# Loading the fourth opening tile of a in one transfer instead of two

## The chip, the cores and the metric

The kernel runs on one core of one Trainium2 chip. The metric is the device time of one execution in microseconds (us); lower is better. Beside the timed runs there is one execution taken by the hardware profiler. Its page and its trace are what is read here: TensorE is PE (its weight loads PEld), VectorE is DVE, ScalarE is ACT, GpSimd is POOL and SyncE is SP. "SPq" is SyncE's queue, from which most plain transfers are issued.

## The reference

With a of 1024 x 1024, b of 1024 x 2048 and c of 2048 x 1024, all float32:

```python
h = np.matmul(a, b)
h = 0.5 * h * (1 + np.tanh(np.sqrt(2 / np.pi) * (h + 0.044715 * h ** 3)))
return np.matmul(h, c).astype(np.float32)
```

Two matrix products with the tanh form of GELU between them.

## The kernel before

The schedule is written by hand: each engine executes its instructions in the order in which the program text issues them to it. A tile has 128 partitions. TensorE contracts over the partitions, so a has to be turned: k on the partitions, rows of a along the free axis (aT). The hidden matrix h is kept turned as well, n on the partitions.

**Opening.** This is where the diff lies. `load_a0(mt, parts)` (L66) allocates a float32 tile of 128 rows and 1024 columns of a (512 KB, 4 KB a row) and loads it from SyncE's queue in `parts` column slices (L70). It is called for the first four row tiles, mt = 0 to 3 (L81). `load_b0(k, parts)` (L73) loads one slice of b: 128 rows of k and the first 1024 columns, also 512 KB, also from SyncE (L77); it is called for all eight k (L83), slice 0 in two halves. The pool for a has four buffers, that for b six, so slices 6 and 7 of b wait until the casts of slices 0 and 1 have freed a buffer. On GpSimd a small copy `gate` (L86) reads slice 4 of b; GpSimd's own loads follow it in that engine's order.

While the loads run, TensorE does `warm_up` matmuls on zeros (L93). `cast_a0(mt)` (L97) makes bfloat16 of a tile: VectorE does columns 0 to 511 (L99), ScalarE columns 512 to 1023 (L100). `turn0(mt, ...)` (L103) transposes the tile in two groups of four 128 x 128 blocks on TensorE (L107) into one of two PSUM buffers `pt`, and copies each group into aT: group 0 on VectorE (L110), group 1 on ScalarE (L112). The order around it is what matters here:

```python
    ab = [cast_a0(0)]
    for mt in R:
        if mt < 3:
            ab.append(cast_a0(mt + 1))
        turn0(mt, ab[mt], (0,) if mt == 3 else (0, 1))
        if mt < 3:
            warm_up(3)
    cast_b0(0)
```

So on VectorE the cast of tile 3 stands ahead of the copy of tile 2's first group, and that copy has to free its `pt` buffer before the first group of tile 3 can be transposed. Group 1 of tile 3 is turned only after the first k group of matmuls.

`cast_b0(k)` (L116) makes bfloat16 of a slice of b, the left 512 columns on VectorE (L117), the right 512 on ScalarE (L118). Then, for each k, six matmuls (L132) add to six PSUM banks: the first 512 rows of a times the first 768 columns of b. All matmuls of one k need slice k.

**The rest.** The six banks go through GELU on ScalarE (L138). GpSimd's queue loads the second half of a, the other columns of b and then c (L150 to L155, L251). The remaining tiles of the first 1024 columns of h are computed plainly (L174 and L167, with more transposes at L160). The last 1024 columns of h, and then all of the second product, use sums and differences of quarter matrices, seven block products in place of eight; those products run in `prod` (L233), with the sums made on VectorE (L197 to L220, L241, L349), ScalarE and by accumulating transfers. Stores go out from SyncE (L345). None of this is touched by the diff.

Of the kernel before, what the change touches and what calls it, by code (L numbers as in the profile page):

```python
# [19 lines left out]
def kernel(ctx, tc, a, b, c, out):  # L20
# [45 lines left out]
    def load_a0(mt, parts):  # L66
        st = astage.tile([128, K], F32, name="a_st")
        w = K // parts
        for i in range(parts):
            nc.sync.dma_start(out=st[:, ts(i, w)], in_=av[:, mt, ts(i, w)])  # L70
        a_st[mt] = st
# [7 lines left out]

    gate = consts.tile([128, 1], F32, name="gate")  # L80
    for mt in R:  # L81
        load_a0(mt, 2 if mt == 3 else 1)
    for k in range(KT):  # L83
        load_b0(k, 2 if k == 0 else 1)

# [349 lines left out]
```

## Time and profile before

| | us |
|---|---|
| median of 4 runs | 121.59 |
| lowest and highest run | 120.63, 122.12 |
| the profiled execution, its whole time | 121.55 |
| its span, from first to last instruction | 119.8 |
| TensorE busy in the span | 112.5 (94%) |
| VectorE busy | 81.7 (68%) |
| ScalarE busy | 46.3 (39%) |

Starts in the trace are counted from the beginning of the span. A row of the timeline gives start, duration, engine, line, operation, out<-in with the shapes, and in brackets how long the engine had been idle before it and which event ended that. Rows that follow each other on one engine can be merged (x3); ends of pipelined instructions are modelled, so neighbours may overlap a little. The "chain that ended last" is followed back from the last instruction: at each step to what released it, or to the instruction before it on its engine.

Some more durations that the steps use: the L70 and L77 issues take 0.33 to 0.81 us each on SyncE's queue (most 0.44), and the transfers of a land 3.4 to 6.3 us after their issue, those of b 6.5 to 9.8 us.

### The profile page before, as it was taken

How to read it: one execution, taken by the hardware profiler on the slowest of the kernel's cores; microseconds unless marked ns; L12 is line 12 of the kernel's file. 1: busy time of each engine (PE TensorE's matmuls, PEld its weight loads, DVE VectorE, ACT ScalarE, POOL GpSimd, SP SyncE). 2: the span in 40 equal slices, each digit the busy share in tenths (PEclk: the TensorE clock that was granted, in tenths of full speed). 3: DMA queues.
4: the chain of work that ended last, by engine and by line, in shares of the span. 5: the costliest groups of instructions: out<-in, count | busy, mean ns of one | idle time of the engine just before them, and what ended most of it. 6: DMA issues, size and time to landing. Idle time of an engine off the chain costs nothing.

```text
span 119.8 us, 1587 instructions
## 1 busy us (share of the span) xinstructions
PE 112.5 (94%) x579; PEld 75.4 (63%) x585; DVE 81.7 (68%) x111; ACT 46.3 (39%) x77; POOL 26.6 (22%) x39
## 2 busy tenths in 40 slices
PE   6966799999999999999999999999999999999990
PEld 2343344469844444788888446888888888886470
DVE  0353233045999945999999999995789992834350
ACT  4355545876533365505359999412000000000000
POOL 2000049923300000066504248200006500000000
PEclk9999999999999999999999999999999999999999
DMA  3999999999999999929999999999997999854434
GB/s 112 369 359 348 419 416 196 188 356 384 215 206 208 206 208 386 321 63 245 257 238 207 190 200 198 183 200 152 149 169 159 242 263 345 327 189 174 167 114 157
DMA packets 13831, 28.41 MB, mean 237 GB/s; under 512 B 1024, under 2 KB 5504, under 8 KB 13824
## 3 DMA queue, kind: packets, MB, share of 16 engines
q0 software_dynamic: 9216, 17.83, 72.3%
q1 hardware_dynamic: 4464, 10.42, 23.3%
q8 instruction: 4, 0.07, 0.2%
q10 hardware_dynamic: 144, 0.07, 0.2%
q14 instruction: 3, 0.02, 0.0%
HBM read 20.97 MB, written 4.19 MB: 210 GB/s over the span
## 4 chain that ended last, share of the span: by engine, by line
PE 86%; DMA 7%; SPq 2%; issue 1%; DVE 1%
PE ps L233 63%; PE ps L174 10%; PE ps L132 8%; DMA b_st<-in_b_dram 7%; PE ps L167 4%; SPq L70 2%; PE pt L160 1%; SPq L77 1%; DVE b_lo L117 0%; DVE ot L404 0%
## 5 line engine op out<-in xcount | busy, mean ns | idle before, releaser
L233 PE MATMUL ps<-t,s 128*128 128x512 f32 x64 | 14.9, 392 | 0.0
L233 PE MATMUL ps<-c,h 128*128 128x512 bf16 (+2 forms) x78 | 14.1, 336 | 0.1
L233 PEld LDWEIGHTS ps<-t,s 128*128 128x128 f32 x64 | 12.0, 188 | 2.6
L174 PE MATMUL ps<-aT,b_lo 128*128 128x512 bf16 x54 | 12.5, 379 | 0.1
L138 ACT ACTIVATE h<-ps 128x512 bf16<-128x512 f32 (+2 forms) x19 | 9.4, 537 | 8.2 <-PE ps L174 6.1
L241 DVE TENSOR_TENSOR ot<-ps,v 128x512 f32<-128x512 f32 x16 | 10.4, 685 | 3.1 <-PE ps L233 3.1
L132 PE MATMUL ps<-aT,b_lo 128*128 128x512 bf16 x47 | 10.7, 379 | 1.6 <-DVE b_lo L117 1.5
L138 ACT ACTIVATE h<-ot 128x512 bf16<-128x512 f32 (+1 forms) x16 | 9.4, 623 | 5.9 <-DVE ot L241 5.9
L233 PE MATMUL ps<-t,h 128*128 128x512 f32 x48 | 11.7, 389 | 0.0
L233 PEld LDWEIGHTS <-h 128*128 128x128 bf16 x80 | 7.1, 98 | 7.0 <-issue 0.5
L349 DVE TENSOR_TENSOR ot<-ps,p 128x512 f32<-128x512 f32 x11 | 7.5, 688 | 5.5 <-PE ps L233 3.1
L233 PEld LDWEIGHTS ps<-t,h 128*128 128x128 f32 x48 | 9.0, 188 | 1.9
L174 PEld LDWEIGHTS <-b_lo 128*128 128x128 bf16 x56 | 5.4, 98 | 6.2
L132 PEld LDWEIGHTS <-b_lo 128*128 128x128 bf16 x48 | 4.4, 98 | 7.2 <-DVE b_lo L117 3.4
L117 DVE CAST b_lo<-b_st 128x512 bf16<-128x512 f32 x8 | 3.4, 426 | 7.0 <-DMA b_st<-in_b_dram 7.0
L251 POOL DMA_DIRECT2D c<-in_c_dram x8 | 6.4, 844 | 6.0 <-DMA b<-in_b_dram 3.8
L233 PE MATMUL ps<-as,bt 128*128 128x512 f32 x32 | 7.6, 396 | 0.0
L233 PE MATMUL ps<-as,b 128*128 128x512 f32 x32 | 7.4, 389 | 0.0
L233 PE MATMUL ps<-c,s 128*128 128x512 f32 x32 | 7.4, 389 | 0.0
L118 ACT ACTIVATE b_lo<-b_st 128x512 bf16<-128x512 f32 x8 | 5.0, 630 | 5.4 <-DMA b_st<-in_b_dram 5.4
L233 PE MATMUL ps<-aT,bx 128*128 128x512 bf16 x31 | 7.0, 379 | 0.1
L382 POOL DMA_DIRECT2D t<-c x4 | 3.5, 1042 | 15.3 <-PE ps L233 14.3
(66 smaller groups left out, 167.2 us busy)
## 6 DMA issues: line engine op xcount, KB each, us to landing
out_dram<-ot SPq DMA_DIRECT2D x15, 256.0 KB, 2.1
b_st<-in_b_dram SPq DMA_DIRECT2D x7, 512.0 KB, 9.0
c<-in_c_dram POOLq DMA_DIRECT2D x6, 512.0 KB, 17.8
t<-c POOLq DMA_DIRECT2D x6, 512.0 KB, 6.7
b<-in_b_dram POOLq DMA_DIRECT2D x2, 1024.0 KB, 10.7
c<-in_c_dram POOLq DMA_DIRECT2D x2, 1024.0 KB, 20.2
t<-t POOLq DMA_DIRECT2D x4, 512.0 KB, 8.6
a_st<-in_a_dram SPq DMA_DIRECT2D x3, 512.0 KB, 4.3
```

What stands on the lines that cost most here:

```text
L70: nc.sync.dma_start(out=st[:, ts(i, w)], in_=av[:, mt, ts(i, w)])
L117: nc.vector.tensor_copy(b_lo[:, k, 0:HW], b_st[k][:, 0:HW])
L118: nc.scalar.activation(b_lo[:, k, HW:W0], b_st[k][:, HW:W0], AF.Copy)
L132: nc.tensor.matmul(ps[t], b_lo[:, k, ts(t, 128)], aT[0][:, k, :], start=(k == 0), stop=(k == KT - 1))
L138: nc.scalar.activation(dst, src, AF.Gelu_apprx_tanh)
L167: nc.tensor.matmul(p, b_lo[:, k, ts(t, 128)], aT[1][:, k, ts(q, 256)], start=(k == 0), stop=(k == KT - 1))
L174: nc.tensor.matmul(p, b_lo[:, k, ts(t, 128)], aT[h][:, k, :], start=(k == 0), stop=(k == KT - 1))
L233: nc.tensor.matmul(p, lhs(t)[:, ts(j, 128)], rhs(t)[:, q], start=(t == 0), stop=(t == n - 1))
L241: tt(ot, p, u, op=ADD)
L251: nc.gpsimd.dma_start(out=dst[:, t:t + 4, :], in_=cv[:, r * NH + t:r * NH + t + 4, ts(q, H)])
L349: tt(ot, p, u, op=ADD)
L382: nc.gpsimd.dma_start(out=t2[i], in_=c21[:, P2[i], :], accum_op=ADD)
```

## The change

Tile 3 of a is loaded by one transfer of 512 KB with rows of 4 KB, where it was loaded by two of 256 KB with rows of 2 KB. The first slice of b is still loaded in two halves. SyncE issues four transfers for a in place of five; nothing else in the text of the kernel differs.

```diff
     gate = consts.tile([128, 1], F32, name="gate")
     for mt in R:
-        load_a0(mt, 2 if mt == 3 else 1)
+        load_a0(mt, 1)
     for k in range(KT):
         load_b0(k, 2 if k == 0 else 1)
```

## The prediction

> **What bounds the kernel now.** I read the chain that ended last first, then the same chain in order of time, then the timeline from 7.5 to 10.9 us and after it, and last the table by stretches.
>
> ```profile
> PE 86%; DMA 7%; SPq 2%; issue 1%; DVE 1%
> ```
>
> The chain is TensorE for 86% of the span. The rest is almost all in the opening, which the same chain shows in order of time (start, us, what):
>
> ```profile
> 4.00 0.04 issue
> 4.05 8.65 DMA b_st<-in_b_dram
> 12.70 0.02 issue
> 12.72 0.44 DVE b_lo L117
> 13.16 0.05 issue
> 13.21 9.24 PE ps L132 x42
> 22.45 0.43 PE ps L174 x2
> ```
>
> The transfer issued at 4.05 is slice 1 of b (load_b0(1)). It lands at 12.70, its first half is cast on VectorE, and from 13.21 TensorE runs to 119 with gaps of some 0.05 us. So the end moves only if slice 1, or a slice behind it, moves, or if TensorE gets to its second k group later than 13.21 for another reason. 42 matmuls take 9.24 us, so one group of six takes 1.32 us. The slices behind slice 1 arrive every 1.27 us (their casts begin at 14.01, 15.27, 16.55, 17.83 and 19.10). Slice 2 would be ready for TensorE at 14.49, group 2 begins at 13.21 + 1.32 = 14.53: the slices keep a lead of 0.04 us that grows by 0.05 per group. Hence a shift of the whole stream moves the end one for one, and a shift of slice 1 alone by at most 0.04.
>
> The other path into the first group is that of tile 3 of a, which the diff touches (start, us, engine, line, ..., idle before and its releaser):
>
> ```profile
> 7.57 0.43 DVE L99 CAST ab<-a_st 128x512 bf16<-128x512 f32 x1 [1.35 <-DMA a_st<-in_a_dram]
> 7.91 0.42 DVE L110 COPY aT<-pt 128x512 bf16<-128x512 bf16 x1
> ...
> 8.25 0.43 DVE L99 CAST ab<-a_st 128x512 bf16<-128x512 f32 x1
> ...
> 8.80 0.42 DVE L110 COPY aT<-pt 128x512 bf16<-128x512 bf16 x1
> ...
> 8.91 0.63 ACT L100 ACTIVATE ab<-a_st 128x512 bf16<-128x512 f32 x1 [0.22 <-DMA a_st<-in_a_dram]
> 8.96 0.81 PE L93 MATMUL ps<-warm 128*128 128x512 bf16 x3
> ...
> 9.60 0.39 PE L107 MATMUL pt<-ident,ab 128*128 128x128 bf16 x4
> 10.03 0.42 DVE L110 COPY aT<-pt 128x512 bf16<-128x512 bf16 x1 [0.80 <-PE pt L107]
> 10.37 0.42 DVE L117 CAST b_lo<-b_st 128x512 bf16<-128x512 f32 x1
> ...
> 10.84 0.39 PE L132 MATMUL ps<-aT,b_lo 128*128 128x512 bf16 x1 [0.85 <-DVE b_lo L117]
> ```
>
> Tile 2 is cast from 7.57; the first half of tile 3 on VectorE at 8.25 and its second half on ScalarE at 8.91, each 0.03 after its landing (8.22 and 8.88: the records of landing, 6.1 and 6.3 us after the issues at 2.12 and 2.59). The first k group starts at 10.84, and with the four transposes behind it TensorE is through at 12.54. Then it waits 0.67 us for slice 1. That wait is the cover of everything done on tile 3's path.
>
> **Part 1: one issue less on SyncE's queue.** Five L70 issues start every 0.47 us from 0.74; dropping one brings each b issue forward by 0.47 us until waits take over. But the queue is far ahead of the data: slice 1 is issued at 4.05 and lands 8.65 later, behind transfers that are already queued. Value on the path: 0. It would count only if the DMA engines ran dry; their busy share is 1.02 to 1.05 in most stretches of one microsecond from 3 to 16 us, and 0.91 and 0.92 from 5 to 7.
>
> **Part 2: larger rows.** Half a tile moves rows of 2 KB, a whole one rows of 4 KB. From tile 2 to the second half of tile 3 the ScalarE casts step from 7.57 to 8.91, 1.34 us for 512 KB in two halves; whole slices of b step by 1.27. So one transfer saves 1.34 - 1.27 = 0.07 us of engine time, and all eight slices, which queue behind it, land 0.07 earlier. This is on the path: -0.07. Here the Trainium skill (DMA: Bandwidth & Descriptors, "Anatomy of one DMA") would promise more: a transfer costs a fixed part of about 2.0 us beside its bytes (it gives this for transfers that GpSimd issues), so one fewer would save up to 2 us if they ran one behind the other. The rows show the halves landing 0.66 apart, far below 2: the fixed part lies under the neighbours' data. By the rule -2.0, by the rows -0.07; I take the rows.
>
> **Part 3: the first half of tile 3 comes later.** The cast L99 waited for half the tile and will wait for all of it. Tile 2's cast began at 7.57, so tile 3's begins at 7.57 + 1.27 = 8.84 in place of 8.25: 0.59 later. Behind it on VectorE, in its own order, is the copy L110 of tile 2, which frees the PSUM buffer for tile 3's transposes. Step by step: L99 at 8.84; L110 0.34 behind (as 7.57 to 7.91): 9.18; done after 0.42: 9.60; transposes 0.05 later (as L110's end at 6.22 to PE at 6.27): 9.65, where the three warm-up matmuls had kept TensorE until 9.60 anyway; L110 of tile 3 after 0.43 (9.60 to 10.03): 10.08; the cast of slice 0 after 0.34: 10.42; the first matmul after 0.47 (10.37 to 10.84): 10.89. The 0.59 shrinks to 0.05 at the first group, and ScalarE's half comes 0.07 earlier (8.84), as does its cast of slice 0's second half (10.95 to 10.88). First group and transposes end by 12.59, and slice 1 is ready at 13.21 - 0.07 = 13.14: 0.55 us of cover are left. Value: 0; without cover, +0.05.
>
> **Part 4: the semaphores shift by one.** The trace's records of SyncE show eight landing semaphores in turn. The ninth and later transfers wait for the one eight before: slice 3 (issued 5.45) for tile 1, slice 4 (7.56) for tile 2, slice 5 (8.24) for the first half of tile 3. With one transfer fewer, slices 3, 4 and 5 wait for tiles 0, 1 and 2 instead, about 0.9, 2.1 and 0.7 us earlier. What is queued behind each on SyncE is only the next slice. Slices 6 and 7 still wait for the casts of slices 0 and 1 to free buffers (issues at 11.61 and 13.38), now 0.07 earlier at most. Slice 4 lands at 16.5, 9 us after its issue, so the wait wasn't what kept it. Its worth is bounded from both sides: if the idle 9% of the engines from 5 to 7 us came from too few queued transfers, 2 x 0.09 = 0.18 us are to be had; if more queued transfers get in each other's way, as much is lost. I take 0, for the engines had six whole transfers ahead of them then. GpSimd's gate (L86) waits for slice 4 and so its loads start 0.07 earlier; none of them ended a wait on TensorE from 22.5 to 119.
>
> **Sum.** -0.07 on the path. The profiled execution took 121.55 us (119.8 of span and 1.75 around it), so 121.48; it lies 0.04 under the median of the runs, 121.59, so 121.52: **121.5 us**.
>
> **Rivals.**
>
> 1. *It gets slower through VectorE's order* (15 in 100). From 4.6 to 7.1 and from 9.0 to 11.3 us many transfers go slowly (GB/s falls to 289 to 330 from some 420). The second spell delays slice 1: it came 1.77 us behind slice 0's second half, 0.50 over the usual step, and that half itself came 1.38 behind the first, 0.70 over. Were that 1.2 us not lost, slice 1 would be ready at 12.0, and tile 3's path decides: TensorE would enter the second group at 12.54 before and 12.59 now, +0.05 against a kernel that had the same luck, 121.6. The switch is at slice 1 ready before 12.59. Against it: it was ready at 13.16 here.
> 2. *More transfers queued early fill the engines* (12 in 100): slices 0 and 1 come 0.2 to 0.6 earlier; 0.55 of cover and 0.07 set the limit, so 120.9 to 121.3.
> 3. *A slow spell falls differently* (11 in 100). One more spell costs what one cost here, 0.6 to 1.2 us: 122.1 to 122.7, and nothing of the change itself would show.
> 4. *The clock falls* (4 in 100). The Trainium skill (TensorE: Matmul & The Clock Gate, "What's actually happening") speaks against anything that makes TensorE wait early: after an idle window of about 3.4 us the clock halves. The row shows waits of 0.85 before the first group and 0.67 after it, a granted clock of 1.00, and this change adds 0.05 to one. By the rule as a threshold: nothing. Were it to happen, a window of 3.4 us at half speed loses 1.7 us: 123.2.
>
> **How the numbers follow.** The forecast itself has 58 in 100, at 121.5, with 121.2 to 121.9 as its own range for the scatter of runs (120.63 to 122.12 singly). For 8 in 10 the range takes in rival 2 from 120.9 and most of rival 3, to 122.4. About 1% is what a measurement of this kernel can tell from no change, 120.4 to 122.8 here. Beyond the upper end lie rival 4 and the worst of rival 3, 0.06; beyond the lower end only rival 2 with luck in the runs, 0.03; within it 0.91.
>
> **What would show each step.** Part 2: L117 for slice 1 at about 12.65, the slices still 1.27 apart, L132's long run from 13.14. Part 3: L99 for tile 3 beside L100 at about 8.84, the transposes L107 at 9.65, the first L132 at 10.89 and TensorE's idle before the second group 0.5 to 0.6. Part 4: L77 issues of slices 3 to 5 at about 4.6, 5.5 and 7.6. The forecast is wrong if the second group starts more than 0.3 from 13.14, or if TensorE shows waits after 22 us that it doesn't show now.

## The result, and the profile after

The changed kernel takes 121.94 us (median of 44 runs, 121.27 to 122.67), the kernel before 121.57 us (63 runs, 120.63 to 122.21). The ratio is 1.0032, with a 95% interval of 1.0020 to 1.0045: slower by about 0.39 us, where the forecast was 0.07 faster. The time lies inside the range that was stated, which was made wide for the scatter of runs and for slow spells; the direction was wrong.

The profiled execution of the changed kernel took 121.58 us, with a span of 119.8; it lies in the quicker quarter of its runs, and so hides the loss. Its chain in order of time (start, us, what) is the one of before, and slice 1 of b still sets the start of TensorE's long run:

```profile
3.60 9.10 DMA b_st<-in_b_dram
12.71 0.02 issue
12.73 0.44 DVE b_lo L117
13.17 0.05 issue
13.22 9.24 PE ps L132 x42
```

Slice 1 is issued 0.45 us earlier than before, as the dropped issue lets it, and lands at the same time: 9.10 us under way in place of 8.65. The timeline of the changed kernel shows the tiles:

```profile
8.00 0.43 DVE L99 CAST ab<-a_st 128x512 bf16<-128x512 f32 x1 [1.99 <-DMA a_st<-in_a_dram]
8.34 0.42 DVE L110 COPY aT<-pt 128x512 bf16<-128x512 bf16 x1
...
9.28 0.63 ACT L100 ACTIVATE ab<-a_st 128x512 bf16<-128x512 f32 x1 [0.17 <-DMA a_st<-in_a_dram]
9.28 0.43 DVE L99 CAST ab<-a_st 128x512 bf16<-128x512 f32 x1 [0.53 <-DMA a_st<-in_a_dram]
...
9.63 0.42 DVE L110 COPY aT<-pt 128x512 bf16<-128x512 bf16 x1
...
11.34 1.47 PE L132 MATMUL ps<-aT,b_lo 128*128 128x512 bf16 x5 [0.85 <-DVE b_lo L117]
...
13.22 2.98 PE L132 MATMUL ps<-aT,b_lo 128*128 128x512 bf16 x13 [0.19 <-DVE b_lo L117]
```

Tile 3's two casts now begin together, 1.28 us after tile 2's, and the first k group 2.06 us behind them, as the steps had it. But tile 2 itself came 0.43 us later than before, so the wait for slice 1 is 0.19 us, not the 0.55 foreseen. That goes with the execution and not with the change: tile 2 landed at 7.98 us in this one and at 7.52 in e1, the same kernel again, where the wait is 0.65; in two executions of the opening of before it landed at 7.54 and 7.90 (before and e3).

One profile says little about a loss of 0.3%. What can be read from all of them is where the time is decided. In six profiled executions (three of the opening of before, three of that of after, with e1, e3, e4 and e12 from below) the time less the start of the second k group is the same within 0.1 us:

| execution | slice 1 lands | second group starts | time | time less start |
|---|---|---|---|---|
| before | 12.70 | 13.21 | 121.55 | 108.34 |
| e12, before again | 12.55 | 13.06 | 121.43 | 108.37 |
| e3, before, halves swapped | 12.75 | 13.26 | 121.58 | 108.32 |
| after | 12.71 | 13.22 | 121.58 | 108.36 |
| e1, after again | 12.83 | 13.34 | 121.71 | 108.37 |
| e4, after, copies first | 13.04 | 13.54 | 121.95 | 108.41 |

So all that differs happens before the second group, and in all six slice 1 was what it waited for. A difference of 0.37 us between the medians then stands for a slice 1 that comes 0.37 us later. This is worked out from the table; no single profile shows the median execution, and the means of the three profiles each differ by half as much, 0.19 us (slice 1 at 12.67 and 12.86). Two of the other kernels below don't fit the column: e7 and e8 have 108.76 and 108.75. In e7 TensorE waited a second time, at 25 us, 0.23 us for a tile of a from GpSimd's queue; e8 lost its 0.4 after VectorE's last instruction.

Where the transfers lose it is in the table by stretches. Columns are the stretch, its length, the busy time of each engine, the granted clock, the busy share of the DMA engines and GB/s. The kernel before:

```profile
6.00:7.00 1.00, 0.73 (x9) 0.62 (x10) 0.22 (x1) 0.58 (x2) 0.00 (x0) 1.00 0.92 289
7.00:8.50 1.50, 0.78 (x7) 0.31 (x5) 0.93 (x3) 0.93 (x2) 0.00 (x0) 1.00 1.04 397
8.50:11.50 3.00, 2.15 (x18) 1.18 (x17) 1.36 (x4) 1.85 (x4) 0.00 (x0) 1.00 1.00 343
4.50:11.50 7.00, 4.92 (x40) 2.82 (x41) 3.19 (x9) 4.23 (x8) 0.00 (x0) 1.00 0.98 340
```

The changed kernel:

```profile
6.00:7.00 1.00, 0.94 (x10) 0.68 (x10) 0.01 (x1) 0.36 (x1) 0.00 (x0) 1.00 1.02 401
7.00:8.50 1.50, 0.45 (x3) 0.02 (x1) 0.50 (x2) 0.50 (x1) 0.00 (x0) 1.00 1.03 273
8.50:11.50 3.00, 1.83 (x16) 1.17 (x17) 1.77 (x5) 2.23 (x5) 0.00 (x0) 1.00 0.97 294
4.50:11.50 7.00, 4.49 (x39) 2.63 (x39) 3.04 (x8) 3.96 (x8) 0.00 (x0) 1.00 0.97 309
```

The stretch from 6 to 7 us, where most of tile 3 is moved, is cured: 401 GB/s in place of 289. The next two are worse: 273 for 397 and 294 for 343. They move the end of tile 3, slice 0's halves and the beginning of slice 1. The engines are as busy as before (last column but one), and slices 1 to 3 are issued by 5.62 us, so packets take longer and none is missing for want of issues. The trace's records of single packets show it: most packets of 2 KB take 84 ns, and of those that began from 7 to 11.5 us, over 100 ns took 9 of 433 in before, 10 of 414 in e12 and 30 of 413 in e3, but 72, 70 and 50 of 256 in after, e1 and e4 (the larger totals include packets of tile 3's halves).

Over the seven microseconds from 4.5 to 11.5 the three executions with the opening of before moved 340, 346 and 342 GB/s, those with the opening of after 309, 307 and 337: on average 25 GB/s less, 0.175 MB in 7 us, and at the 418 GB/s that follow, 0.42 us. That is of the size of the loss, but it doesn't follow it from one execution to the next: e4, with 337, has the latest slice 1 of the six. One reason can be seen. The trace records each landing sixteen times, once for each DMA engine, and the cast of slice 1 begins 0.02 us after the last; that last engine lay 1.85 us behind the first in before and 1.43 in after.

### The profile page after: what moved, and what is told of

It reads as the page before. It is cut to its first block, busy times and chain, and to the rows that moved or that the text cites. A ratio compares the mean times of both kernels' runs of the same rounds, so it can differ in the third digit from the quotient of the medians.

```text
span 119.8 us, 1586 instructions
## 1 busy us (share of the span) xinstructions
PE 112.6 (94%) x579; PEld 75.5 (63%) x585; DVE 81.5 (68%) x111; ACT 46.3 (39%) x77; POOL 26.6 (22%) x39
## 4 chain that ended last, share of the span: by engine, by line
PE 86%; DMA 8%; SPq 2%; DVE 1%; issue 1%
PE ps L233 63%; PE ps L174 10%; PE ps L132 8%; DMA b_st<-in_b_dram 8%; PE ps L167 4%; PE pt L160 1%; SPq L70 1%; SPq L77 1%; DVE b_lo L117 0%; DVE ot L404 0%
## 5 line engine op out<-in xcount | busy, mean ns | idle before, releaser
L132 PE MATMUL ps<-aT,b_lo 128*128 128x512 bf16 x47 | 10.7, 379 | 1.1 <-DVE b_lo L117 1.0
L132 PEld LDWEIGHTS <-b_lo 128*128 128x128 bf16 x48 | 4.4, 98 | 6.7 <-DVE b_lo L117 2.9
L93 PE MATMUL ps<-warm 128*128 128x512 bf16 x17 | 5.9, 491 | 1.2 <-DVE warm L50 1.2
```

The source lines that it names most:

```text
L93: nc.tensor.matmul(ps[N0 - 1], warm[:, 0:128], warm, start=True, stop=True)
L132: nc.tensor.matmul(ps[t], b_lo[:, k, ts(t, 128)], aT[0][:, k, :], start=(k == 0), stop=(k == KT - 1))
```

## The experiments

Four accounts are named in what was expected (there called theories). A: VectorE's order, the later cast that holds back the copy behind it. B: the count of opening transfers, with which more of b is queued early. C: the larger rows, or the one piece, of tile 3. D: slow transfers wherever the stream steps between rows of 4 KB and of 2 KB. Ratios are to the kernel before, run on the same chip, with 95% intervals.

| run | what it is | ratio | interval |
|---|---|---|---|
| e1 | after, again | 1.0027 | 0.9997 to 1.0057 |
| e2 | tile 0 in halves, tile 3 whole | 1.0115 | 1.0079 to 1.0150 |
| e3 | before, halves swapped | 0.9997 | 0.9980 to 1.0015 |
| e4 | after, copies of tile 2 first | 1.0029 | 1.0009 to 1.0049 |
| e5 | after, one small transfer more | 1.0015 | 0.9998 to 1.0031 |
| e6, e14 | before, slice 0 whole | 0.9933, 0.9930 | 0.9909 to 0.9957, 0.9904 to 0.9955 |
| e7, e18 | after, tile 3 in rows of 2 KB | 1.0013, 1.0030 | 0.9994 to 1.0032, 1.0013 to 1.0047 |
| e8 | tiles 2 and 3 in halves | 1.0025 | 1.0008 to 1.0042 |
| e9, e15 | after, slice 0 whole | 0.9954, 0.9946 | 0.9931 to 0.9978, 0.9924 to 0.9967 |
| e10 | tile 2 in halves, tile 3 whole | 1.0027 | 1.0003 to 1.0051 |
| e11 | before, all of b in halves | 1.0038 | 1.0019 to 1.0058 |
| e12 | before, again | 0.9991 | 0.9971 to 1.0011 |
| e13 | after, a little of b read first | 1.0068 | 1.0043 to 1.0093 |
| e16 | e9, a little of b read first | 1.0009 | 0.9989 to 1.0030 |
| e17 | tile 3 in halves by partitions | 1.0225 | 1.0163 to 1.0287 |

**e1, the changed kernel again**

> The changed kernel itself, for another profile and another ratio. Theory A (VectorE's order: the later cast of tile 3 holds back the copy of tile 2 and with it the first k group) and theory B (the count of transfers: with one fewer, slices 3 to 5 of b are queued one landing earlier and the transfers disturb each other more) both expect 1.003 of before, 121.9 us. In the profile A expects the first k group at about the time at which ScalarE and VectorE cast tile 3 plus 2.05 us; if this execution is one of the slower ones, A expects the second k group to start without waiting for slice 1, B expects it to wait for a slice 1 that lands later than 12.7 us.

1.0027, 121.78 us. The profiled execution waited for a slice 1 that landed at 12.83, and the slow stretches lie where they lay in the first profile:

```profile
6.00:7.00 1.00, 1.00 (x11) 0.66 (x10) 0.08 (x1) 0.43 (x1) 0.00 (x0) 1.00 0.98 393
7.00:8.50 1.50, 0.66 (x6) 0.25 (x5) 0.76 (x2) 0.95 (x2) 0.00 (x0) 1.00 0.91 261
8.50:11.50 3.00, 2.15 (x18) 1.15 (x17) 1.52 (x4) 1.60 (x4) 0.00 (x0) 1.00 0.96 267
```

**e2, tile 0 split in place of tile 3**

```diff
-        load_a0(mt, 1)
+        load_a0(mt, 2 if mt == 0 else 1)
```

> Tile 0 of a in two halves, tile 3 in one: 14 opening transfers as before, with the same turn of the semaphores from slice 0 on, but tile 3 whole. Theory A (VectorE's order) expects no help: 1.003 of before, 121.9 us. Theory B (the count of transfers) expects 1.000, 121.55 us.

1.0115, far more than either expected. It has a cost of its own: tile 1 landed late (its slowest engine at 7.65 us, 2.4 after its quickest), TensorE stood for 1.95 us, and its granted clock was 0.50 from 9.4 to 12.9 us. The stretches of the transfers are like those of after (389 GB/s from 6 to 7; 302 from 8.5 to 11.5, but 401 between). It says that splitting an earlier tile doesn't restore the time; for the count alone it is no clean test.

**e3, the halves in the other order**

```diff
-        for i in range(parts):
+        for i in reversed(range(parts)):
             nc.sync.dma_start(out=st[:, ts(i, w)], in_=av[:, mt, ts(i, w)])
```

> The kernel before, its two halves of tile 3 issued in the other order: count, sizes and semaphores as before, but VectorE's half lands last. Theory A expects the time of the changed kernel, 1.003 of before, 121.9 us, with the VectorE cast of tile 3 some 0.6 us after the ScalarE cast's landing. Theory B expects 1.000, 121.55 us.

0.9997. VectorE's cast of tile 3 began at 9.24 us, 1.32 after tile 2's, as late as in after (1.28), and the time is that of before. Account A falls here: the late cast costs nothing.

**e4, the copies ahead of the casts**

```diff
-        if mt < 3:
+        if mt < 2:
             ab.append(cast_a0(mt + 1))
         turn0(mt, ab[mt], (0,) if mt == 3 else (0, 1))
+        if mt == 2:
+            ab.append(cast_a0(mt + 1))
```

> The changed kernel, with the copies of tile 2 issued ahead of the casts of tile 3 on VectorE and ScalarE: tile 3 still comes in one transfer, but nothing stands behind its cast that doesn't need it. Theory A expects the loss back: 1.000 of before, 121.55 us, or a little under. Theory B expects 1.003, 121.9 us.

1.0029: the order is repaired and the loss stays. The timeline of e4 (its L134 is L132 of before):

```profile
8.84 0.43 DVE L110 COPY aT<-pt 128x512 bf16<-128x512 bf16 x1 [0.47 <-PE pt L107]
...
9.18 0.42 DVE L99 CAST ab<-a_st 128x512 bf16<-128x512 f32 x1
...
13.06 0.43 DVE L117 CAST b_lo<-b_st 128x512 bf16<-128x512 f32 x1 [2.21 <-DMA b_st<-in_b_dram]
...
13.54 2.76 PE L134 MATMUL ps<-aT,b_lo 128*128 128x512 bf16 x12 [0.93 <-DVE b_lo L117]
```

The copy stands ahead of the cast, VectorE idles 2.21 us for slice 1 and TensorE 0.93. It is the transfers that are late.

**e5, a fourteenth transfer that nothing reads**

```diff
     for mt in R:
         load_a0(mt, 1)
+    pad = consts.tile([1, H], F32, name="pad")
+    nc.sync.dma_start(out=pad, in_=a[0:1, 0:H])
```

> The changed kernel with a fourteenth opening transfer, one row of 2 KB that nothing reads, issued from SyncE where the second half of tile 3 stood. Tile 3 still comes whole. Theory B (fewer transfers: the b issues move up on SyncE and slices 3 to 5 are queued one landing earlier) expects the loss back: 1.000 of before, slice 1 landing at about 12.7 us. Theory C (the larger rows of tile 3, or tile 3 in one piece, disturb the transfers, whatever the count) expects 1.003.

1.0015, between the two and apart from neither. From 7 to 8.5 us its profile has 262 GB/s and from 8.5 to 11.5 305, as in after; slice 1 landed at 12.58 all the same, since the stretch ahead was a quick one (412 GB/s from 4.5 to 6). Inconclusive.

**e6 and e14, slice 0 of b whole, tile 3 in halves**

```diff
     for mt in R:
         load_a0(mt, 2 if mt == 3 else 1)
     for k in range(KT):
-        load_b0(k, 2 if k == 0 else 1)
+        load_b0(k, 1)
```

> The kernel before, tile 3 in two halves, with slice 0 of b in one transfer instead: 13 opening transfers, as many as in the changed kernel, in which slices 3 to 5 of b wait for tiles 0 to 2. Theory B (the count) expects 1.003 or more. Theory C (rows of tile 3) expects 1.000. A late first k group, about 0.5 us later than before since VectorE waits for the whole of slice 0, still fits under slice 1 and is expected to cost nothing by itself.

> Tile 3 of a in two halves, slice 0 of b whole, a second time: 0.993 of before (0.991 to 0.996 the first time). If tile 3 whole costs something only ahead of the halves of slice 0, this and the next one agree within 0.2%.

0.9933 and 0.9930, 120.68 and 120.90 us: faster than before and after, with the 13 transfers that account B called too few. B falls in the form in which it was stated, that fewer transfers are slower whichever they are. The chain of e14 no longer has slice 1 in it; tile 2 starts it and TensorE enters the second group without a wait:

```profile
1.64 6.07 DMA a_st<-in_a_dram
...
12.47 0.22 PE pt L107 x4
12.69 9.06 PE ps L132 x42
```

**e7 and e18, one transfer with rows of 2 KB**

```diff
+        if mt == 3:
+            wide = consts.tile([128, 2, 520], F32, name="a_st")
+            nc.sync.dma_start(out=wide[:, :, 0:512],
+                              in_=av[:, mt, :].rearrange("p (g w) -> p g w", g=2))
+            a_st[mt] = wide
+            return
```

(Cut: in `cast_a0` the two casts of tile 3 read the two halves of `wide`.)

> The changed kernel, tile 3 in one transfer but into a tile whose two halves lie 32 bytes apart, so that it moves rows of 2 KB as the two halves did. Theory C in its form of row sizes expects 1.000 of before; theory B (the count of transfers) expects 1.003 or a little more, 121.9 us.

> Tile 3 in one transfer with rows of 2 KB, a second time (1.0013, 0.9994 to 1.0032 the first). Theory D expects GB/s near 400 from 7 to 8.5 us and 1.000 to 1.001 of before; the count of transfers expects 1.003.

1.0013 and 1.0030; weighted by their intervals 1.0022, 1.0010 to 1.0035. From 7 to 8.5 us the two profiles have 385 and 313 GB/s, from 8.5 to 11.5 261 and 273, no better than after. The smaller rows by themselves don't bring the time back, so the rows aren't what the two halves were good for. (For the time this rests on e18: the interval of e7 reaches both 1.000 and 1.003, and its profile has the second wait named above.)

**e8, e10 and e11, other splits**

```diff
e8:  load_a0(mt, 2 if mt >= 2 else 1)
e10: load_a0(mt, 2 if mt == 2 else 1)
e11: load_b0(k, 2)
```

> The kernel before with tile 2 in two halves as well: 15 opening transfers, slices of b issued another 0.47 us later and slice 2 waiting for tile 0's landing no more than the next ones for theirs. Theory B, if it goes on in the same way, expects 0.997 to 1.000 of before; theory C expects 1.000 plus 0.07 us for the smaller rows, 121.6 us.

> Tile 2 of a in two halves, tile 3 whole: 14 opening transfers as before, but rows go 4, 2, 4, 2, 4 KB in place of 4, 2, 4. Theory D expects two more slow spells than before: tile 3's landings spread over the engines by more than 1.2 us, slice 1 at 12.9 us or later, 1.003 to 1.010 of before. Theory B (the count) expects 1.000.

> The kernel before with every slice of b in two halves, so that rows of 2 KB go on from tile 3 to the end of b and there is one step instead of two. Theory D expects no slow spell from 9 to 11 us, so slice 1 some 0.4 us earlier than in before, at about 12.3, but every slice takes 1.34 instead of 1.27 us, 0.5 us in all at slice 7, and 7 more issues; the time between 0.998 and 1.004. If the spell from 9 to 11 stays, it belongs to the first reading of b and not to the row size.

e8 took 1.0025: more transfers are no gain. e10, with tile 3 whole, took 1.0027, and its slice 1 landed at 13.73 in the profile, with tile 3 spread over the engines by 2.06 us, as D expected; the count alone did not bring the time back. e11 took 1.0038, and from 8.5 to 11.5 us it moved 303 GB/s although its rows of 2 KB go on: the slow stretch at the beginning of b is not a step in the row size. That is against D.

**e9 and e15, both whole**

> Tile 3 of a and slice 0 of b both in one transfer: 12 opening transfers, all with rows of 4 KB. Theory D (the transfers go slowly for about a microsecond where the stream steps between rows of 4 KB and of 2 KB; with tile 3 whole this step falls on the first slice of b) expects the slow spells from 6 to 7 and from 7 to 9 us gone, slice 1 landing at 12.2 us or earlier, and 0.993 of before or less. Theory B (fewer transfers queue more of b early and disturb more) expects it slower than the kernel with slice 0 alone whole: over 0.995. The reading of b for the first time may still cost a spell at 9 to 11 us, by either.

> Tile 3 and slice 0 both whole, a second time: 0.995 of before (0.993 to 0.998 the first time). If tile 3 whole costs 0.3% whatever follows, this is 1.003 of the kernel with tile 3 in halves and slice 0 whole.

0.9954 and 0.9946 (after with `load_b0(k, 1)`, as in e6). There is no row of 2 KB left in the opening, and the stretches of e9 are

```profile
6.00:7.00 1.00, 1.00 (x11) 0.60 (x10) 0.24 (x2) 0.59 (x3) 0.00 (x0) 1.00 1.01 410
7.00:8.50 1.50, 1.50 (x15) 0.88 (x13) 0.97 (x3) 1.32 (x3) 0.00 (x0) 1.00 1.06 412
8.50:11.50 3.00, 2.15 (x13) 1.01 (x12) 1.21 (x4) 1.44 (x3) 0.00 (x0) 1.00 0.87 273
```

The stretches from 6 to 8.5 are quick, as D had it; the one from 8.5 to 11.5 is not (273 here and again in e15), where the kernels with tile 3 in halves and slice 0 whole have 311 and 378. Yet slice 1 landed no later for it: at 11.58 and 12.03 us in e9 and e15, at 12.06 and 11.61 in e6 and e14. In e6, e14 and e15 it is not slice 1 that TensorE waits for in the end, but the tiles of a. Weighted, tile 3 whole makes 0.9950 of 0.9932: 1.002, with an interval from about 0.999 to 1.004. That fits the loss of the change, and doesn't exclude none.

**e12, the kernel before again**

> The kernel before itself, for a second profile and as a measure of the scatter: 1.000 of before. Theory D expects GB/s near 400 from 7 to 8.5 us and a slow spell from 6 to 7 and from 9 to 11, as in the first profile. If the spells lie elsewhere, they are not tied to the row sizes.

0.9991. Its stretches of 277, 380 and 351 GB/s repeat the 289, 397 and 343 of the first profile: the pattern belongs to the kernel, not to the one execution. The repeats of other kernels agree less well (e6 and e14 have 311 and 378 in the last of these stretches, e7 and e18 385 and 313 in the middle one).

**e13 and e16, a few rows of b read ahead of all**

```diff
+    touch = consts.tile([32, H], F32, name="touch")
+    nc.sync.dma_start(out=touch, in_=b[0:256, :].rearrange("(p s) n -> p s n", s=8)[:, 0, 0:H])
```

> The changed kernel with one more transfer ahead of all: 64 KB, every eighth row of slices 0 and 1 of b, 2 KB of each, which nothing reads; 0.17 us of the engines. If the slow spell at the beginning of b (7 to 11 us) comes from addresses of b being read for the first time, it shrinks and slice 1 lands up to 0.7 us earlier: 0.996 of before. If it comes from the halves of slice 0 or from where the row size steps, it stays, and the time is that of the changed kernel plus 0.1 to 0.2: 1.003 to 1.005.

> Tile 3 and slice 0 both whole, with the same early 64 KB of b ahead of all. No 2 KB rows follow each other in the stream after that. If the spell at 8 to 11 us belongs to the first reading of b, it shrinks and the time is 0.3% under that of the kernel without it, 0.992 of before; if not, it is 0.1% over it, 0.996.

1.0068 and 1.0009, each 0.4 to 0.6% over its kernel without the touch and above both of the times expected for it; why the touch costs so much isn't shown. The slow stretch stays (271 and 287 GB/s from 8.5 to 11.5). That an address of b is read for the first time is not its cause, as far as one row in eight can tell.

**e17, tile 3 in halves by partitions**

```diff
+        h = 128 // parts
         for i in range(parts):
-            nc.sync.dma_start(out=st[:, ts(i, w)], in_=av[:, mt, ts(i, w)])
+            nc.sync.dma_start(out=st[ts(i, h), :], in_=av[ts(i, h), mt, :])
```

> Tile 3 in two transfers of 64 partitions each: 14 opening transfers and twice 256 KB as before, but whole rows of 4 KB. If the rows of 2 KB are what helped (theory D), the slow spell from 7 to 8.5 us is there as in the changed kernel (GB/s under 300) and the time is 1.003 of before. If the count of transfers is what helped, 1.000 and GB/s of 380 or more from 7 to 8.5.

(With `parts` = 2 slice 0 of b keeps its column halves; only load_a0 is edited.) 1.0225, by a cost of its own: the two transfers of 64 partitions landed at 8.64 and 9.88 us, 1.24 apart where column halves are 0.66 apart, and TensorE's clock then fell to half for two spells of 3.4 us. As a test of the count it fails. Of its stretches, 223 GB/s from 7 to 8.5 is the slow spell that D expected, but the two slow transfers fall into it; 372 from 8.5 to 11.5 is as in the other kernels with tile 3 in two transfers.

**Taken together.** From 8.5 to 11.5 us the profiles of kernels with tile 3 in two transfers have 343, 351, 343, 348, 303, 311, 378 and 372 GB/s (before, e12, e3, e8, e11, e6, e14, e17), those with tile 3 in one 294, 267, 313, 305, 302, 295, 273, 273, 261, 273, 271 and 287 (after, e1, e4, e5, e2, e10, e9, e15, e7, e18, e13, e16): means of 344 and 285, with a small overlap. So the start of b goes slower behind a whole tile 3, whatever the rows. That is shown as a difference between two groups of profiles, in a stretch that was chosen with the profiles in view; over the whole of 4.5 to 11.5 us the means are 341 and 323 and overlap widely (330 to 355, 291 to 344).

Slice 1 itself, where slice 0 comes in halves, landed at 12.26 to 12.88 us in the six profiles with tile 3 in two transfers (mean 12.67) and at 12.58 to 13.73 in the nine with tile 3 in one (mean 13.10; four of these kernels differ from after by a split or a transfer more, e2, e5, e10 and e13). Where slice 0 is whole, no such difference is seen (e9 and e15 above). So what is shown is narrow, and as a difference between groups: behind a whole tile 3 the halves of slice 0 go slower, and slice 1 comes later. What in the chip makes it so isn't shown: neither the row size, nor the first reading of b, nor a lack of queued transfers explains it.

## Why the prediction was wrong

**Part 1** (one issue less, worth 0) held: slice 1 was issued 0.45 us earlier and landed no earlier.

**Part 2** is the step that failed: "one transfer saves 1.34 - 1.27 = 0.07 us of engine time, and all eight slices, which queue behind it, land 0.07 earlier". The rate of the stream was taken from two quiet places and the rest was held to be the same on both sides. The slices do follow at 1.27 us in after. But between tile 3 and slice 1 the stream is not quiet, and the change altered how it goes there: slice 1 landed 0.19 us later by the means of three profiles each, and 0.37 later if the medians of all runs are put down to it, where 0.07 earlier was expected. There is a gain from 6 to 7 us, where tile 3 went at 401 GB/s in place of 289, more than the rows were to bring. It was given back with more on slice 0. Nor did one transfer less gain anything like the 2.0 us that Part 2 weighed and set aside. Why slice 0 goes slower then stays open. (The sentence ahead of this part, that a shift of slice 1 alone moves the end by at most 0.04, holds only for an earlier slice 1: a later one holds up TensorE by the whole of its delay.)

**Part 3** (VectorE's order, worth 0) held. The chain of 2.05 us from tile 3's casts to the first group was found at 2.06; e3 shows that the late cast alone costs nothing, e4 that putting the copy first wins nothing. The cover varied with tile 2, which the working had fixed at its old time: 0.19 us in after and 0.65 in e1, 0.55 having been stated.

**Part 4** (semaphores, worth 0, at most 0.18 either way) had the waits right (slices 3 to 5 were issued at 4.60, 5.62 and 7.99, the last behind tile 2, which came late). Its worth stays open: e5 undoes the shift and has half of the loss, but its interval reaches both ends. It is not the whole account, since e6 has the same shift and is the fastest of all.

Of the **rivals**, the first fell with e3 and e4 as an explanation of the loss, though its path is real: as soon as slice 0 whole brings slice 1 forward, tile 2 and tile 3 decide (e6, e14, e15). The second did not come: more was queued early, and slice 0 landed no sooner (its second half at 10.98 us, 10.93 in before). The third was the nearest: it had slow spells of 0.6 to 1.2 us that fall differently. It erred in "nothing of the change itself would show", that is, in holding the spells for chance. The second profile of before shows that they stand at the same places, and that was to be had from no single profile. The fourth did not happen in after. The sign by which the forecast was to be called wrong, a second group more than 0.3 us from 13.14, was too coarse for an effect of this size: the profile of after has 13.22, close to the forecast by the luck of a quick execution, and of the three with the opening of after only e4, at 13.54, passes it.

## What to carry to other kernels

A stream of transfers that looks full at one rate can run 10 to 40% slower for a few microseconds, at places that repeat in part from run to run and differ with how the transfers ahead are cut (261 to 378 GB/s here in place of 418); an estimate of bytes by the quiet rate says nothing of these, so an opening that waits on a stream needs its cuts tried in combination, and against several profiles. Find which landing TensorE waits for and judge a cut by that landing alone: here, slice 0 of b in one transfer with tile 3 still in two was worth 0.7%, far more than the edit under study, and it showed the next limit, the tiles of a. When the loss is of the size of the scatter, relate the total time to one event in the trace (here the start of the second group) over all profiles, and compare groups.

## What the runs showed of the hardware that was not expected

In the one profile of e17, a half transfer over 64 of the 128 partitions took nearly as long as a whole one: 1.24 us between landings for 256 KB, against 0.66 for column halves of the same size and 1.27 for 512 KB.

The granted clock fell without an idle spell of 3.4 us. In these traces it changes in steps of 3.41 us. In e2, TensorE was busy for 1.45 of the 3.4 us ahead of such a step, with a longest wait of 1.95, and in e17 for 1.55; both ran on at half the clock:

```profile
6.00:9.40 3.40, 1.45 (x13) 0.78 (x12) 1.20 (x4) 1.55 (x3) 0.00 (x0) 1.00 1.04 383
9.45:12.85 3.40, 3.28 (x17) 1.82 (x15) 1.20 (x4) 2.48 (x5) 0.00 (x0) 0.50 0.95 329
7.49:10.90 3.41, 1.55 (x14) 0.97 (x14) 1.52 (x4) 2.04 (x4) 0.00 (x0) 1.00 1.04 321
10.92:17.72 6.80, 5.95 (x21) 2.37 (x20) 2.77 (x7) 3.69 (x8) 1.38 (x3) 0.50 1.02 410
```

(Two rows of e2, then two of e17.) In after, the emptiest such window (7.86 to 11.27) had 1.67 us busy and kept the full clock, and in before 1.85. The Trainium skill (TensorE: Matmul & The Clock Gate, "What's actually happening") lets the clock fall after an idle window of about 3.4 us; here a window with over four tenths of work was enough, and the prediction's fourth rival, which took the idle time as the threshold, set it too high. In these traces the line lies between 1.55 and 1.67 us of work in such a window; no run narrows it further.
